# A rotation by 180 degrees on one core: a strip loaded first, and an early zero write to rows that the last store overwrites

## The chip, the cores and the metric

One core of a Trainium2 chip. The metric is the device time of one execution in microseconds. The kernel before takes 123.19 us (median of 3 runs, 123.14 to 123.35).

## The reference

```python
def setup_inputs():
    return {"x": np.random.randn(32, 3, 256, 256).astype(np.float32)}

def reference(x):
    return np.rot90(x, k=2, axes=(-2, -1)).astype(np.float32)
```

96 planes of 65,536 floats, each reversed end to end: 25.17 MB in, 25.17 MB out, no arithmetic.

## The kernel before

The 96 planes are three groups of 32. A group is 128 rows of 16,384 floats (64 KB): four rows to a plane, one row to a partition. A group is loaded whole, every row is reversed by DVE, and the store puts the four rows of each plane down in reversed order.

```python
    x4 = x.rearrange("b c h w -> (b c) (h w)").rearrange(
        "(g n) (s e) -> g (n s) e", n=G, s=4)
    o4 = out.rearrange("b c h w -> (b c) (h w)").rearrange(
        "(g n) (s e) -> g n s e", n=G, s=4)
    # ... buffers A, Bt, Ct of 64 KB a partition, T of 8 KB; cut
    def load(t, g, lo=0, hi=E):
        nc.sync.dma_start(out=t[:, lo:hi], in_=x4[g][:, lo:hi])

    def store(t, g):
        nc.sync.dma_start(out=o4[g][:, ::-1, :], in_=t[:, :])
    # across(dst, src): four DVE copies, reversed, from one buffer to another; cut
    # inside(t): twelve DVE copies that reverse a buffer in place through T; cut

    load(A, 0)
    load(Bt, 1)
    across(Ct, A)
    store(Ct, 0)
    load(A, 2)
    inside(Bt)
    store(Bt, 1)
    across(Ct, A)
    store(Ct, 2)
```

Of the kernel before, what the change touches and what calls it, by code (L numbers as in the profile page):

```python
# [2 lines left out]

os.environ.setdefault("NEURON_RT_ULTRASERVER_MODE", "4")

# [4 lines left out]


@with_exitstack
def kernel(
    ctx: ExitStack,
    tc: tile.TileContext,
    x: bass.AP,
    out: bass.AP,
):








    nc = tc.nc
    P = 128

    B, C, H, W = x.shape
    L = H * W
    G = 32
    E = L // 4
    K = E // 4
    J = E // 8

    x4 = x.rearrange("b c h w -> (b c) (h w)").rearrange(
        "(g n) (s e) -> g (n s) e", n=G, s=4)
    o4 = out.rearrange("b c h w -> (b c) (h w)").rearrange(  # L40
        "(g n) (s e) -> g n s e", n=G, s=4)

    pool = ctx.enter_context(tc.tile_pool(name="slots", bufs=1))
    A = pool.tile([P, E], x.dtype, tag="A")
    Bt = pool.tile([P, E], x.dtype, tag="B")
    Ct = pool.tile([P, E], x.dtype, tag="C")
    T = pool.tile([P, J], x.dtype, tag="T")

    def back(t, lo, hi):
        return t[:, hi - 1:(lo - 1 if lo else None):-1]  # L50

    def copy(dst, src):
        tc.keep_in_program_order(nc.vector.tensor_copy(out=dst, in_=src))  # L53
# [7 lines that stand above are left out]
    def across(dst, src):  # L61
        for c in range(0, E, K):
            copy(dst[:, c:c + K], back(src, E - c - K, E - c))

    def inside(t):
        for lo in range(0, E // 2, J):
            hi = E - lo - J
            copy(T[:, :], back(t, hi, hi + J))
            copy(t[:, hi:hi + J], back(t, lo, lo + J))
            copy(t[:, lo:lo + J], T[:, :])  # L70

    load(A, 0)
    load(Bt, 1)
    across(Ct, A)
    store(Ct, 0)
# [7 lines that stand above are left out]
# [1 line left out]
_INS = ['x']  # L84
_OUTS = [((32, 3, 256, 256), 'float32')]


# [23 lines left out]
```

## Time and profile before

| | before |
|---|---|
| time, span in the profile | 123.19 us, 121.26 us |
| one DMA queue's share of 16 engines' span | 97.3% |
| DVE busy | 27% |
| a normal packet (65,536 B) on one DMA engine | 2.418 us |

Each of the 16 DMA engines carries six transfers of eight packets, back to back. A *round* is one packet on each of the 16 engines, a *turn* is the place where the queue changes from loads to stores or back, and a *ring* is the queue of one issuing engine, q1 of SyncE and q10 of ACT on the pages below. Where a packet takes longer than 2.42 us, I call the difference its *excess*; averaged over the 16 engines, it is 0.67 us in the first packets of the first load and 1.12 us in the last packets of the second load, just ahead of the first store. I call the latter "the slow round". The lines of the page and of the stretches stand in the prediction. They are cut so that each stretch holds one packet of every engine; a packet's bytes and its time count where it starts. The same holds for the DMA row of the page: a low digit says that few packets start in that slice, not that the engines stand still.

### The profile page before, as it was taken

How to read it: one execution, taken by the hardware profiler on the slowest of the kernel's cores; microseconds unless marked ns; L12 is line 12 of the kernel's file. 1: busy time of each engine (PE TensorE's matmuls, PEld its weight loads, DVE VectorE, ACT ScalarE, POOL GpSimd, SP SyncE). 2: the span in 40 equal slices, each digit the busy share in tenths (PEclk: the TensorE clock that was granted, in tenths of full speed). 3: DMA queues.
4: the chain of work that ended last, by engine and by line, in shares of the span. 5: the costliest groups of instructions: out<-in, count | busy, mean ns of one | idle time of the engine just before them, and what ended most of it. 6: DMA issues, size and time to landing. Idle time of an engine off the chain costs nothing.

```text
span 121.3 us, 72 instructions
## 1 busy us (share of the span) xinstructions
DVE 32.5 (27%) x20; POOL 0.2 (0%) x4
## 2 busy tenths in 40 slices
DVE  0000000599300079999100000009990000000000
POOL 0000000000000000000000000000000000000000
DMA  9777977997899497799789977997798779877980
GB/s 346 346 346 346 692 346 346 389 649 346 346 432 605 195 497 346 346 605 432 346 346 605 432 346 346 627 411 346 346 649 389 346 346 649 389 346 346 670 368 0
DMA packets 864, 50.33 MB, mean 415 GB/s; under 512 B 96, under 2 KB 96, under 8 KB 96
## 3 DMA queue, kind: packets, MB, share of 16 engines
q1 hardware_dynamic: 864, 50.33, 97.3%
HBM read 25.17 MB, written 25.17 MB: 415 GB/s over the span
## 4 chain that ended last, share of the span: by engine, by line
DMA 59%; DVE 13%; DVEq 2%; SPq 1%; issue 0%
DMA A<-in_x_dram 59%; DVE Ct L53 13%; DVEq L106 2%; SPq L59 1%; DVEq L53 0%
## 5 line engine op out<-in xcount | busy, mean ns | idle before, releaser
L53 DVE COPY Ct<-A 128x4096 f32<-128x4096 f32 x8 | 17.8, 2288 | 46.3 <-DMA A<-in_x_dram 46.3
L53 DVE COPY T<-Bt 128x2048 f32<-128x2048 f32 x4 | 4.9, 1228 | 11.7 <-DMA Bt<-in_x_dram 11.6
L53 DVE COPY Bt<-Bt 128x2048 f32<-128x2048 f32 x4 | 4.9, 1227 | 0.1
L53 DVE COPY Bt<-T 128x2048 f32<-128x2048 f32 x4 | 4.9, 1226 | 0.1
L95 POOL MEMSET const-bfloat16-1.0<- 128x1 bf16 x1 | 0.1, 102 | 0.0
L95 POOL MEMSET const-uint8-127<- 128x1 uint8 x1 | 0.1, 101 | 0.0
L95 POOL MEMSET const-float32-0.0<- 128x1 f32 x1 | 0.1, 99 | 0.2 <-issue 0.2
L95 POOL MEMSET const-float32-1.0<- 128x1 f32 x1 | 0.1, 98 | 0.0
## 6 DMA issues: line engine op xcount, KB each, us to landing
A<-in_x_dram SPq DMA_DIRECT2D x2, 35.7
out_dram<-Ct SPq DMA_DIRECT2D x2, 30.3
Bt<-in_x_dram SPq DMA_DIRECT2D x1, 41.9
out_dram<-Bt SPq DMA_DIRECT2D x1, 42.9
```

What stands on the lines that cost most here:

```text
L53: tc.keep_in_program_order(nc.vector.tensor_copy(out=dst, in_=src))
L59: nc.sync.dma_start(out=o4[g][:, ::-1, :], in_=t[:, :])
L95: nc = _bacc.Bacc("TRN2", target_bir_lowering=False, num_devices=1)
L106: with _tile.TileContext(nc) as tc:
```

## The change

Its intent, as far as the text shows it: a strip of 2 KB of every row goes first, so that the engines start on short packets; and 512 B of every output row of the last group are written with zeros at once, on ACT's ring, so that the output has been written to early. The last store overwrites the zeros.

```diff
+    Z = 128
+    N = E // 32
+    z4 = out.rearrange("b c h w -> (b c) (h w)").rearrange(
+        "(g n) (s e) -> g (n s) e", n=G, s=4)
 ...
-    load(A, 0)
+    zeros = T[:, 0:Z]
+    nc.vector.memset(zeros, 0.0)
+    load(A, 0, 0, N)
+    load(A, 0, N, E)
+    nc.scalar.dma_start(out=z4[2][:, 0:Z], in_=zeros)
     load(Bt, 1)
```

## The prediction

> **What bounds the kernel now.** I read the page first: engines, then the queue, then the slices. DVE is busy 27% of the span and no other engine computes, while the one DMA queue is busy for nearly all of it:
>
> ```profile
> span 121.3 us, 72 instructions
> DVE 32.5 (27%) x20; POOL 0.2 (0%) x4
> DMA  9777977997899497799789977997798779877980
> ...
> q1 hardware_dynamic: 864, 50.33, 97.3%
> ```
>
> Columns of the last line: packets, MB, share of 16 engines' span. 50.33 MB is the whole input read once and the whole output written once, so no byte can be saved. The lone "4" in the DMA row (slice 14, about 39.4 to 42.5 us) is the only weak slice between the first and the last. Next, does the queue ever wait for DVE? The SyncE waits and the timeline answer it:
>
> ```profile
> SPq L106 <- DMA out_dram<-Ct: 19.3, 1, 19.3
> ...
> 31.50 0.63 SPq L59 DMA_DIRECT2D out_dram<-Ct  x1
> ...
> 58.22 0.55 SPq L59 DMA_DIRECT2D out_dram<-Bt  x1
> ...
> 90.86 0.54 SPq L59 DMA_DIRECT2D out_dram<-Ct  x1
> ```
>
> The timeline's columns are start and length of the issue in us. In the trace's packet records the three stores' first packets start near 42.4, 81.1 and 100.4 us, so each store was issued about 10 to 23 us before its turn. DVE is off the path, and the chain of waits on the page (which goes through DVE copies) is not what sets the end. What sets it is the slowest of the 16 DMA engines, each of which carries 6 transfers x 8 packets of 65,536 B without a gap.
>
> So I cut the span at packet boundaries (columns: stretch, length, DVE, POOL, clock, DMA share, GB/s):
>
> ```profile
> 0.00:1.70 1.70, 0.00 (x0) 0.20 (x4) 1.00 0.00 0
> 1.70:4.70 3.00, 0.00 (x0) 0.00 (x0) 1.00 1.03 350
> 4.70:7.10 2.40, 0.00 (x0) 0.00 (x0) 1.00 1.01 437
> 36.20:38.60 2.40, 0.00 (x0) 0.00 (x0) 1.00 1.01 437
> 38.60:42.10 3.50, 0.00 (x0) 0.00 (x0) 1.00 1.01 300
> 42.10:44.50 2.40, 1.38 (x2) 0.00 (x0) 1.00 1.01 437
> ```
>
> Each stretch from the second on holds one packet per engine (16 x 65,536 B). The normal round takes 2.4 us at 437 GB/s. Two rounds don't: the first load's first packet (3.0 us) and the last packet of the second load, just ahead of the first store (3.5 us). The packet records say it per engine: a normal packet is 2.418 us and the pace is 19.319 us for eight, 2.415 each. The first packets start between 1.74 and 2.70 us and take 2.60 to 3.31 us. The last packets of the second load take 3.30 to 3.97 us, a mean of about 1.13 us too much, on all 16 engines together. No later turn between load and store, in either direction, has such a packet (largest 2.494 us). The engine that ends the kernel (its last landing record at 120.12 us) is the one with the largest stall, 3.969 - 2.419 = 1.55 us. From there to the end of the span is 1.14 us, and from the span to the measured time 123.19 - 121.26 = 1.93 us.
>
> Budget: start to first packet 1.94, first packet 3.02, 46 normal ones 46 x 2.415 = 111.09, the stalled one 3.97, tail 1.14: 121.16 of 121.26; the rest is semaphore packets and a 0.08 us slow packet at 79 us.
>
> **What the Trainium skill says.** "DMA: Bandwidth & Descriptors", section "Where 436 GB/s comes from", gives 16 ports x 32 B x 850 MHz = 435 GB/s as the ceiling; the full rounds above, at about 435, agree. So the normal packets can't get faster, and only the two slow rounds and the start are to be had. The same page, "Issuing engines are not separate DMA queues": what ACT issues runs on the same 16 engines and interleaves with SyncE's. This trace has no ACT transfer, so it can't say. Its section "Queues, rings and completion order" says that an engine takes turns between rings at packet boundaries, and that a DMA's semaphore is the ordering one has; so the 512 B zero packets will be mixed into the first load, and the overwriting store must wait for the zeros' semaphore, which will be some 95 us old by then. "HBM Reference", section "Latency", has 0.2 us on average and 2 us at high load; the two engines that started last show a first packet of 2.604, 0.19 us over normal, which fits the 0.2. No page that I found speaks of a stall at the first write to a tensor; that reading of the 3.5 us round is my own inference.
>
> **The change, part by part.** The intent must be the two slow rounds. The engines that began at 1.74 us waited longest and those that began at 2.5 to 2.7 us hardly at all, as if one thing, ready at about 2.6 us, let all reads go. The 3.5 us round looks like the same for the output's first write. The zero write makes that first write at 2 to 3 us, where engines stand still anyhow.
>
> - *Removed: the stall at 38.6 to 42.1.* Taking each engine's excess off its own end, the last engine is then the one that started at 2.70 us: its last packet ends near 119.72, with 0.89 us of stall, so 118.83. Against 120.12 this is a gain of 1.29 us, not 1.55, because another engine becomes the last.
> - *Added: the strip.* The same bytes in 16 packets per engine rather than 8 for the first load. A packet's fixed share is 2.415 - 65,536 B / 27.2 B per ns (the skill's 435 by 16, an estimate) = 6 ns, up to 10. Eight more packets and a 9 ns semaphore packet: 0.06 to 0.1 us. It also adds a SyncE issue of about 0.4 us (the first two took 0.38 and 0.42) but eight strip packets (8 x 2,048 B / 27.2 = 0.6 us) cover that. The first packet's latency is paid as before; I see no direct gain from the strip, other than that zeros need not wait behind a 2.4 us packet.
> - *Added: the zeros.* 8 packets per engine of 512 B: 19 ns of bytes plus 10 ns, 0.24 us at least; I take 0.3 as an estimate, since short writes may cost more. The memset of 128 elements on DVE, by the copies' 1.23 us for 2,048, is under 0.1 us, beside other work. ACT's issue then comes at about 1 us; SyncE's first took 1.0 us from issue to first packet, so zeros move from about 2.1 us on.
> - *Moved: the first write's stall.* If it is still about 1.1 us from about 2.1 us on, it ends at 3.2 to 3.4, where reads flow from 2.6 to 2.9. If it blocks the engine, as it blocked a load's packet in the kernel before, some 0.5 us stays exposed; if it blocks only its own ring, none. I take 0.3.
> - *Unmoved:* DVE's copies, whose slack is 10 us; T is needed again only at 43 us.
>
> Sum: -1.29 + 0.1 + 0.3 + 0.3 = -0.6, so 122.6. I say **122.5**, leaning a little to a fuller hiding.
>
> **Rivals.** (a) *The stall is hidden fully*, with zero packets running inside the wait for the first read: -1.29 + 0.1 = 122.0, and 121.7 if the strip also lets the late engines start sooner (their 0.3 us). For it: the read stall is there anyway. Against: engines that start late have no idle time to give. (b) *The stall is not about the first write* but about the first load-to-store turn on SyncE's ring, or hits each region of the output when it is first touched, and the zeros touch the wrong one. Then it stays at about 39 us and the added packets cost 0.2 to 0.6: 123.4 to 123.8. Against: stores to the second and third part show no stall in the kernel before, so one first touch serves the whole output. (c) *It is given back in full*: the stall comes at the start and blocks all engines one after the other with the read stall: -1.29 + 1.13 + 0.4 = 123.4. For it: it was a load's packet that was lengthened, so such a stall can hold up other work on the engine. (d) *Zeros are far dearer than their bytes*, say 0.2 us each: 8 x 0.2 = 1.6 less the 0.3 assumed puts it at 123.8.
>
> **Range and chances.** (a) gives the low end, (b) and (c) the high: 121.7 to 123.5. A gain over 2% needs 120.73, a cut of 2.46 us; taking out both slow rounds whole (1.3 and at most 0.9) doesn't reach it. A loss of 2% needs 125.65, which only (d) several times over could bring. Hence 0.02, 0.96, 0.02.
>
> **What would show it.** Right: no round over 2.5 us near 39 us, all later rounds near 2.4 us at 435 GB/s, a first load that lands later than 22.55 us by 0.3 to 0.8 us, and the second load's landing at 43.07 coming forward by over 0.5 us. Wrong: a 3.5 us round that is still just ahead of the first store (b); the first load landing later by over 1.2 us (c, d); or a first load that lands no later than before (a). DVE on the path at any store would refute the whole frame.

## The result, and the profile after

123.1 us (median of 4 runs, 123.05 to 123.2) against 123.16 (4 runs, 123.02 to 123.35); the ratio is 0.9995, interval 0.9977 to 1.0012. The time is the same. It lies inside the stated range of 121.7 to 123.5, but 122.5 was forecast, a gain of about 0.7 us, and there is none. The page of the changed kernel (slices of 3.03 us, the two queues and their issues):

```profile
span 121.3 us, 79 instructions
...
DMA  4977997998889297799789977997798779877980
...
q1 hardware_dynamic: 1008, 50.33, 97.2%
q10 hardware_dynamic: 144, 0.07, 0.2%
...
out_dram<-T ACTq DMA_DIRECT2D x1, 64.0 KB, 2.9
```

The zeros are queue q10, 144 packets: 128 of data and 16 of the semaphore, landed 2.9 us after their issue. The weak slice, "4" before, is now a "2", at the same place, slice 14: a few packets fewer happen to start in it, so this is no sign of a longer stall. The stretches of the changed kernel (stretch, length, DVE, POOL, clock, DMA share, GB/s) show the slow round itself:

```profile
36.20:38.60 2.40, 0.00 (x0) 0.00 (x0) 1.00 1.01 437
38.60:42.20 3.60, 0.00 (x0) 0.00 (x0) 1.00 0.97 291
42.20:44.60 2.40, 1.28 (x2) 0.00 (x0) 1.00 1.01 437
```

The slow round is untouched. Its packets take 3.26 to 3.90 us, mean excess 1.09 us against 1.12. And the zeros had met no stall of their own. From the packet records of the changed kernel (times in us from the start of the span; the records don't name their engine; a packet is taken to follow the one at whose end it starts):

```
strip packets (2,048 B):  first at 1.74; 95 of the 128 take 0.081 to 0.087, the others up to 0.87
zero packets (512 B):     128 of them, from 2.73 to 3.53, every one 0.027 long, 0.0234 from start to start
first long packets:       start at 2.92 to 3.53, mean excess 0.04
semaphores of the zeros:  landed 3.26 to 3.89
last of the first load:   landed 22.79 (22.55 before)
second load:              landed 43.16 (43.07 before)
last semaphore packet:    starts at 120.07 (120.12 before), landed 120.46 (120.46 before)
```

So the output was written, and the write confirmed, by 3.9 us, in 27 ns a packet, and the turn at 39 us cost what it had cost before.

### The profile page after: what moved, and what is told of

Its sections match the earlier page's. It is cut to its first block, busy times and chain, and to the rows that moved or that the text cites. A ratio compares the mean times of both kernels' runs of the same rounds, so it can differ in the third digit from the quotient of the medians.

```text
span 121.3 us, 79 instructions
## 1 busy us (share of the span) xinstructions
DVE 32.7 (27%) x21; POOL 0.2 (0%) x4
## 3 DMA queue, kind: packets, MB, share of 16 engines
q1 hardware_dynamic: 1008, 50.33, 97.2%
## 4 chain that ended last, share of the span: by engine, by line
DMA 58%; DVE 13%; DVEq 2%; SPq 1%; issue 0%
DMA A<-in_x_dram 58%; DVE Ct L62 13%; DVEq L119 2%; SPq L68 1%; SPq L65 0%; DVEq L62 0%
```

## The experiments

Eighteen kernels. Those executed once are judged by their records. "Before" in a comparison is the kernel before on the same chip.

**The first four: later, earlier, on the other ring, to other rows.**

```diff
 # e1_reload
     load(Bt, 1)
+    load(Bt, 1)
 # e2_store_first
-    load(Bt, 1)
     across(Ct, A)
     store(Ct, 0)
+    load(Bt, 1)
 # e3_zeros_sp (the change, without the strip)
-    load(A, 0, 0, N)
-    load(A, 0, N, E)
-    nc.scalar.dma_start(out=z4[2][:, 0:Z], in_=zeros)
+    load(A, 0)
+    nc.sync.dma_start(out=z4[2][:, 0:Z], in_=zeros)
 # e4_zeros_g0 (the change)
-    nc.scalar.dma_start(out=z4[2][:, 0:Z], in_=zeros)
+    nc.scalar.dma_start(out=z4[0][:, 0:Z], in_=zeros)
```

> The kernel before with the second load issued twice, so the first store comes one load later (about 63 to 64 us instead of 42.4; the second load waits for the first's semaphore, some 2 us of empty queue near 43 us). Theory TURN (the slow round belongs to the last load packet before the first store, whatever the time): no packet over 2.6 us near 39 us, and packets of 3.3 to 4.0 us near 60 to 63 us. Rival CLOCK (something at a fixed time, 39 to 42.8 us after the start): 3.3 to 4.0 us at 39 us as before, nothing near 61 us. Rival ADDRESS (the last rows of the second load's data are slow to read): 3.3 to 4.0 us in both places.

> The kernel before with the second load moved behind the first store, so that the queue is empty from 22 to about 33 us and the store is then followed by loads; about 10 us slower. TURN: no packet over 2.6 us at 39 to 43 us; the stall shows at the store's first packet (3 us or more) or not at all, as no load is ahead of it. CLOCK: the packet that covers 39 to 42.8 us takes 3.3 to 4.0 us though it is a store's or the load's first. ADDRESS: the last packet of the moved load, about 69 us, takes 3.3 to 4.0 us.

> The change without the strip, and the zeros issued by SyncE between the first and the second load, to the same rows of the last group. RING (a form of TURN: the first store on SyncE's own ring costs it, and ACT's ring did not count): the last packet of the first load, about 18 to 22 us, takes 3.3 to 4.0 us, and the one at 39 us 2.42. If it is not the ring (region or time or size): 39 us slow as before, 2.42 at 20 us.

> The change with the zeros written to the first group's rows, those that the first real store writes, instead of the last group's. REGION (each region of the output costs at its first touch and the change touched the wrong one): the round at 39 us falls from 3.5 to 2.42 us and the time to about 122.0 to 122.5. All other theories: the slow round stays, 123.1 us.

*e1* and *e2* were inconclusive: the framework's scheduler moved the instructions. In e1 SyncE issued the store ahead of the repeated load (142.67 us), in e2 its instruction order came out as that of the kernel before (123.07 us), so e2 is a repeat of it. The moral is to look at the order of the built program first; the later runs either pin it or, as their issues in the trace show, came out in the order written.

*e3*: 123.52 us, before 123.34. With the zeros between the first and second load on SyncE's own ring there is no packet over 2.6 us near 20 us, and the slow round at 39 us keeps a mean excess of 1.02 us. *e4*: 122.99 us, before 123.34, slow round 1.12 us. So it is neither the ring nor the rows: the theory that the first write pays, whichever form, had no support left at this size of write.

**What the slow round goes with: time, address or place.** The loads and stores are now pinned to program order (a wrapper round both `dma_start` calls, except in e6, whose issues came out in the order written).

```diff
 # e5_delay
+    nc.vector.memset(A[:, :], 0.0)
     load(A, 0)
 # e6_groups_120: groups handled in the order 1, 2, 0
 # e7_store_in_order: e2's edit, pinned
 # e8_three_loads: e1's edit, pinned
```

> The kernel before with the loads kept in order behind a DVE memset of the whole buffer A, so that every transfer starts some 8 to 17 us later (call it D). CLOCK (a fixed time after the start): the slow round stays at about 38.7 to 42.7 us, now four to seven packets earlier in the second load, and the kernel takes 123.2 + D. PLACE (anything tied to what the queue does: packet count, turn, address): the slow round moves to 38.7 + D.

> The kernel before with the three groups handled in the order 1, 2, 0. ADDRESS OF THE INPUT (the last rows of group 1 are slow to read): the slow round moves to the last packets of the first load, about 18.6 to 22 us. Otherwise it stays at 38.7 to 42.7 us and the time at 123.2.

> What e2_store_first was meant to be (there the scheduler put the load ahead again): the second load is kept behind the first store, the queue is empty from 22 to about 33 us, time about 133. TURN: the first store's first packet, near 33 us, takes over 3 us, or nothing does, since no load packet is ahead of it; none near 39 us. CLOCK: the packets that cover 39 to 42.7 us, the first store's third and fourth, are slow by about 1 us. PACKET COUNT (after 16 data packets on an engine): the last packet of the store, about 50 us, is slow.

> What e1_reload was meant to be: two loads into the second buffer in order, then the first store, some 2 us empty near 43 us, time about 144.5. TURN: the slow round is just ahead of the first store, near 60 to 64 us, and none at 39. CLOCK, PACKET COUNT and ADDRESS: it stays at 38.7 to 42.7 us; ADDRESS has it again at 60 to 64 us, for the same rows are read again.

*e5* (140.26 us): everything begins 17.2 us later, and so does the slow round, at 55.8 to 60.0 us with 1.08 us. No fixed time. *e6* (123.0 us): the slow round stays at 38.7 us with 1.10 us although other rows are read there. No address of the input. *e8* (144.8 us), its stretches:

```profile
38.60:41.00 2.40, 0.00 (x0) 0.00 (x0) 1.00 1.01 437
57.90:60.30 2.40, 0.00 (x0) 0.00 (x0) 1.00 1.01 437
60.30:63.90 3.60, 0.00 (x0) 0.00 (x0) 1.00 0.99 291
63.90:66.30 2.40, 1.34 (x2) 0.00 (x0) 1.00 1.01 437
```

Nothing at 39 us now. The slow round (1.14 us) sits in the last packet of the third load, ahead of the first store, which has moved there. It belongs to the first turn from loads to stores. (The third load had to wait for the second to land. No packet runs for 1.28 us near 42 us, and the third load's first packets have 0.72 us of excess. Gaps like this are taken up below.)

*e7* (134.37 us) fitted no theory neatly. Its first store finds an empty queue and its first packets have 0.08 us of excess: a first big write on its own is not slow. But the turn from that store to the load behind it cost 0.75 us in the store's last packet (and 0.40 us in the next packet on eight engines), and the next turn, load to store near 92 us, 0.55. In the kernel before the same kind of turn, store to load at 62 us, costs nothing.

**Pattern, size, number of turns, two rings.**

```diff
 # e9_plain_store (wrong result on purpose: rows not exchanged)
-        nc.sync.dma_start(out=o4[g][:, ::-1, :], in_=t[:, :])
+        nc.sync.dma_start(out=z4[g], in_=t[:, :])
 # e10_big_zeros (the change, without the strip)
-    Z = 128
+    Z = E // 8
 # e11_more_turns: load(Bt,1), load(A,2) and all stores in column halves, pinned, in the order
 #   load A | load Bt lo | store | load Bt hi | store | load A lo | store | load A hi | store store store
 # e12_store_act
-        nc.sync.dma_start(out=o4[g][:, ::-1, :], in_=t[:, :])
+        nc.scalar.dma_start(out=o4[g][:, ::-1, :], in_=t[:, :])
```

> The kernel before with stores that write the rows in the order of the buffer's partitions (a wrong result on purpose), so that store and load split over the engines alike. PATTERN (the slow round is the price of the store's reversed three-level pattern, or of its other split over the engines): no packet over 2.6 us at 38.7 to 42.8 us, time about 122. TURN of any kind: slow round unchanged, mean excess 1.0 to 1.1 us, time 123.1 to 123.3.

> The change without the strip and with zeros of 8 KB a row instead of 512 B (1 MB, through ACT's ring, beside the first load). FIRST WRITE, ONLY TOO SMALL BEFORE: the 39 us round falls to 2.42 us and packets of the first load show the 1 us instead; about 125.5 (2.4 us of bytes more, less 0, as the cost moves). TURN: the 39 us round keeps its 1.0 to 1.1 us; about 125.6 to 126.

> The kernel before with the second and third load and all stores in column halves, so that SyncE's ring turns from load to store three times and back twice or more. EVERY TURN COSTS: 0.5 to 1.1 us of excess at each of the turns to a store (about 32, 52 and 71 us), time 125 or more. FIRST TURN ONLY: about 1.1 us at the first turn, near 29 to 32 us, under 0.2 us at the others, time 123.2 to 123.5.

> The kernel before with the stores issued on ACT's ring, so that no ring turns and loads and stores alternate packet by packet from about 32.5 us on. TURN WITHIN A RING: no slow round at all, about 122.0. FIRST LARGE STORE, whatever ring: packets with about 1 us of excess near 32 to 36 us, time 123.0 to 123.3. MIXING costs more than the turn: many packets over their pace, over 123.5.

*e9* (123.16 us, before 123.08; its result is wrong): slow round 1.22 us; the store's pattern doesn't matter. *e11* (123.26 us), stretches at the first, second and third turn to a store:

```profile
29.00:30.30 1.30, 1.30 (x2) 0.00 (x0) 1.00 0.98 378
30.30:32.20 1.90, 1.23 (x1) 0.00 (x0) 1.00 1.08 276
32.20:33.50 1.30, 0.00 (x0) 0.00 (x0) 1.00 1.00 429
50.60:51.80 1.20, 0.00 (x0) 0.00 (x0) 1.00 1.02 437
69.90:71.10 1.20, 0.00 (x0) 0.00 (x0) 1.00 1.01 437
```

Packets are 32 KB here and a normal one takes 1.213 us; the first stretch misses one of the 16 packets of its round. The first turn costs 0.13 and 0.84 us in two rounds, 0.97 together; the second 0.01 us near 50.8 us, the third nothing near 70 us, the fourth 0.07 us near 90 us. The price is paid once, not per turn.

*e12* (123.16 us median of 4 runs, 123.02 to 124.3; ratio 1.0036, interval 0.9983 to 1.0089): with the stores on ACT's ring the slow round comes as soon as the first store joins, in the load packets that start at 33.8 to 34.4 us, 1.24 us, and never again, though from there loads and stores alternate packet by packet. Not a matter of one ring.

*e10* (125.4 us): here an early write did change something. With 8 KB a row, mixed into the first load, the turn costs 0.44 us instead of 1.1, but the load's packets that start near 21.5 us, behind which two zero packets follow each other, have 0.31 us of new excess, and the zeros' own 8 x 0.309 = 2.47 us come on top. So size counts: 512 B pieces leave the turn as it is, 8 KB pieces lower it. But most of that is moved, not saved: over all rounds from the second to the turn the excess is 0.88 us, against 1.15 in the kernel before.

**Paid once per kernel, or once per stretch of work in the queue?** This decides what the price is. For the gap, the third load waits until the first store has landed.

```diff
 # e13_idle_between (pinned): the third load goes to C, behind a memset of C
-    load(A, 2)
     inside(Bt)
+    nc.vector.memset(Ct[:, :], 0.0)
+    load(Ct, 2)
     store(Bt, 1)
-    across(Ct, A)
-    store(Ct, 2)
+    across(A, Ct)
+    store(A, 2)
 # e17_short_gap: e13 without the memset
 # e18_gap_same_buffers (pinned): the kernel before, and
-    load(A, 2)
     inside(Bt)
+    nc.vector.memset(Ct[:, 0:8], 0.0)
+    nc.vector.memset(A[:, 0:8], 0.0)
+    load(A, 2)
```

> The kernel before with the third load put into buffer C behind a memset of C, so that the queue stands empty from about 62 to 77 us; then a load of 19.3 us turns to the second store near 97 us. STREAM STATE (an empty queue undoes what the first turn paid): 0.7 to 1.2 us of mean excess in the load's last packet near 93 to 97 us, besides the 1.1 us near 39 us. ONCE PER KERNEL (something that is touched once): under 0.2 us near 97 us. Total about 138 to 140 us either way.

> e13_idle_between without the memset of C: the third load into C still waits for the first store to land, so the queue is empty for 1.5 to 2.5 us near 62 us, and the turn to the second store comes near 83 us. If any empty moment resets the stream: 0.5 us or more of mean excess in the load's first packets near 64 us and 0.7 to 1.4 us in its last near 81 to 84 us, total about 126 to 127 us. If only a long rest does: under 0.2 us near 83 us, total about 125 us.

> The kernel before with its own buffers; two memsets of 8 elements make the third load (into A) wait until the first store has landed, so the queue is empty for 1 to 2 us near 62 us. If the gap is what brings the price back: 0.5 to 0.7 us of mean excess in the third load's first packets and 1.0 to 1.4 us in its last, near 81 to 85 us, total about 127. If the buffer did it in e17_short_gap: under 0.2 us at the turn, total about 125.2.

In the kernel before, the second load-to-store turn, at 81 us, costs nothing (one packet of 2.494 us). The stretch with the eight rounds of the third load, from just behind the first store to that turn:

```profile
61.40:80.70 19.30, 0.00 (x0) 0.00 (x0) 1.00 1.00 435
```

*e13* (143.96 us): the queue is empty from 62 to 80 us. Then the load's first packets have a mean excess of 0.56 us, as at the start of the kernel, and its last packets, at the turn to the second store, 1.40 us. *e17* (126.93 us, before 123.17): a gap of 1.30 us between the last packet of the store and the first of the load is enough, 0.53 and 1.24 us. *e18* (127.83 us, before 123.31) has the buffers of the kernel before and the gap alone; its stretches:

```profile
62.40:63.90 1.50, 0.08 (x2) 0.00 (x0) 1.00 0.00 0
63.90:66.80 2.90, 0.00 (x0) 0.00 (x0) 1.00 1.06 362
66.80:69.20 2.40, 0.00 (x0) 0.00 (x0) 1.00 1.01 437
78.90:81.30 2.40, 0.00 (x0) 0.00 (x0) 1.00 1.01 437
81.30:85.00 3.70, 0.00 (x0) 0.00 (x0) 1.00 1.01 283
85.00:87.40 2.40, 0.68 (x1) 0.00 (x0) 1.00 1.01 437
```

An empty stretch, a slow first round (0.66 us), normal ones, and a slow round at the next turn (1.33 us). So nothing is "touched once". An empty queue of 1.3 to 1.5 us brings both prices back, long after the first third of the output had been written. The time adds up: in e18 an engine stands idle for 2.64 us on average and then loses 0.66 and 1.33 us, 4.63 together, and the kernel is 4.52 us slower.

Three checks from the records. The pinning isn't the cause: e5 is pinned and has no gap at this place, and its second load-to-store turn has 0.01 us of excess. The length of the load ahead of the turn isn't either: in e1 two loads, 16 packets on each engine, run without a gap between the first and the second store, and that turn has 0.03 us. And the price of the restart is that of a load: in e7 the first packets behind a gap of 10.6 us are a store's, with 0.08 us.

**Where the cost of the added packets went.**

```diff
 # e14_strip_only: the change without the memset and the ACT store
 # e15_zeros_only: the change with load(A, 0) whole
 # e16_early_piece: no zeros; the last 8 KB of each row of group 0 loaded first,
 #   reversed, and stored through ACT's ring during the rest of the load
```

> The change without zeros. If the strip has no use of its own: eight packets of 84 ns and one semaphore packet in place of 8 x 76 ns cut from the long ones, 0.07 us later on every engine and 123.1 to 123.3. If it draws the engines' starts together (the change's spread of 0.52 us after the slow round against 0.62 before): 0.1 to 0.2 us faster, 122.9 to 123.0.

> The change without the strip. The zeros' packets are 8 x 27 ns and 9 ns on each engine, 0.23 us, and nothing hides them: 0.2 us slower, 123.3. If the zeros wait in the shadow of the first read: no change.

> No zeros; the last 8 KB of every row of the first group are loaded first, reversed and stored through ACT's ring while the rest of the load runs; no added bytes. If early mixing pays part of the first turn, as e10_big_zeros hints (excess at the turn 0.44 instead of 1.1, and 0.31 elsewhere): 122.7 to 123.0. If not: 123.2 to 123.4, for the added packets.

Against the kernel before (median of 11 runs 123.09 us): *e14* 123.01 us (6 runs), ratio 0.9999 (0.997 to 1.0028); *e15* 123.28 us (6), 1.001 (0.9987 to 1.0032); *e16* 122.93 us (6), 0.9985 (0.9958 to 1.0013). None is told from the kernel before by its time. The packet records tell a little more. Means over the 16 engines of one profile each, us from the start of the span; the first three rows do the same work up to this point, so they show the scatter:

| kernel | packet ahead of the turn starts | its excess | ends | latest engine's end |
|---|---|---|---|---|
| before | 38.87 | 1.12 | 42.41 | 42.77 |
| e2 (= before), e6, e9, e13 | 38.93, 38.90, 38.81, 38.87 | 1.01, 1.10, 1.22, 1.15 | 42.35, 42.42, 42.46, 42.43 | 42.67, 42.79, 42.82, 42.72 |
| e1, e17, e18 (= before up to the turn) | 38.95, 38.90, 38.82 | 1.04, 1.24, 1.39 | 42.41, 42.57, 42.63 | 42.93, 42.99, 43.60 |
| e14, strip alone | 38.77 | 1.30 | 42.49 | 42.74 |
| e15, zeros alone | 39.04 | 1.07 | 42.53 | 42.78 |
| after, e4 (both) | 39.02, 39.01 | 1.09, 1.12 | 42.52, 42.55 | 42.80, 42.73 |

With the zeros, alone or with the strip, the packet ahead of the turn starts at 39.01 to 39.04 us, later than in any of the first eight (38.81 to 38.95, mean 38.88): the added packets do cost the average engine about 0.14 us. With the strip alone it starts at 38.77, a little ahead of all eight. But at the end of the slow round nothing can be told apart any more: every excess and every mean end lies in the range of the eight (1.01 to 1.39, 42.35 to 42.63). That the strip's saving was paid back at the turn, with 1.30 us, is therefore not shown. At the end of the kernel the latest engine, which sets the time, is not later: its last packet ends at 120.08 us (after) and 120.03 (e4), against 120.07 to 120.24 in before, e2, e6 and e9, and the ends of the 16 engines lie within 0.52 and 0.53 us instead of 0.70 to 0.78. *e16* has the shape of e10: 0.72 us at the turn, 0.31 us new in the first load's last packets, and 1.24 us over all rounds up to the turn, no less than the kernel before's 1.15. The price was spread, not lowered.

No version beat the kernel before clear of noise.

## Why the prediction was wrong, point by point

- **What bounds the kernel**: right. DMA packets back to back, DVE aside; the changed kernel's queue has 97.2% of the span. Two readings were off without weight in the sum: 120.12 us is the last packet, the last landing was at 120.46; and the 0.19 us of the two engines that started last, set beside a latency of 0.2 us, is no constant, for in e1, e5, e8 and e12 the engine that started last has no excess (2.415 us).
- **"Removed: the stall at 38.6 to 42.1", -1.29 us**: this step failed. It rested on "the 3.5 us round looks like the same for the output's first write", marked as an inference. The zeros wrote to the output at 2.7 to 3.5 us at 27 ns a packet, and the slow round stayed, with 1.09 us instead of 1.12: the term measured -0.03 us, within the scatter. In its place the runs show a price of 1.0 to 1.4 us for the first large turn between loads and stores after the queue was empty (e5, e8, e11, e18); in e7, where the queue restarts with a store, it is split over two turns. The argument that misled me was sound as far as it went, "no later turn has such a packet", but once per kernel and once per unbroken run of the queue look alike in a kernel whose queue never runs dry. Only a gap could tell them apart.
- **"Moved: the first write's stall", +0.3 us**: there was nothing to move. The zeros ran from 2.73 us, not 2.1, at 27 ns each, and the first long packets behind them have 0.04 us of excess: no stall is seen beyond that of the first reads.
- **"Added: the zeros", 0.3 us**: 8 x 27 ns and a 9 ns semaphore packet, 0.225 us by the lengths of the records, or about 0.19 by their starts, 23.4 ns apart; near the 0.24 worked out. The mean engine came to the turn about 0.14 us later, the latest engine ended the kernel no later. The memset took 0.17 us, not under 0.1, beside other work.
- **"Added: the strip", 0.06 to 0.1 us**: 8 packets of 84 ns and 9 ns more, less 8 x 76 ns cut from the long ones, 0.07 us by the lengths, or about 0.04 by the starts, 80 ns apart. No such cost can be seen: with the strip alone (e14) the engines came to the turn 0.1 us sooner. Its "no direct gain" is right in the time.
- **The sum**: -0.6 became -0.06 in the medians, which is noise. Rival (b), that the stall is the first turn and stays, named the right event, though it isn't bound to SyncE's ring (e12), but put the time at 123.4 to 123.8, since it added the packets' cost to the engine that ends last. The latest of the 16 engines, with which the kernel ends, was not delayed: their spread at the end was 0.52 us instead of 0.70. Why the spread shrank is open.
- **The chances and the signs**: 0.96 for within 2% came out, and the time lies in the range, but neither speaks for the mechanism: the range's high end was made of rivals (b) and (c), in which nothing is gained. The second load landed 0.09 us later instead of over 0.5 earlier, the first 0.24 later (0.3 to 0.8 forecast). The observable that I named as fatal to the step ("a 3.5 us round that is still just ahead of the first store") is what the profile showed.

What stays open: why the first turn costs 1.0 to 1.4 us and later ones do not, what holds that state, why pieces of 512 B leave it as it is while 8 KB pieces spread it over earlier rounds, and what sets the split in e7. The runs with a gap (e13, e17, e18) were executed once each. Whether start and turn share one fixed sum is not shown either.

## What to carry to other kernels

A cost that a kernel shows once may be paid once per kernel or once per unbroken run of the queue; before building a warm-up for it, put a gap in and see whether it comes back. In a kernel bound by the DMA engines, don't let the queue run empty in mid-kernel: here gaps of 1.3 and 1.5 us (e17, e18) cost 1.8 and 2.0 us more in the rounds behind them. And read the packets of all 16 engines: the end is set by the latest, so a small cost on the mean engine can be free, and a small gain too.

## What the Trainium skill lacked or had wrong

- "DMA: Bandwidth & Descriptors", section "Latency and other measured facts" (and no other page that I found): nothing on the first change between loads and stores after an empty queue. Here it took 1.0 to 1.4 us on the mean of 16 engines, in the packet ahead of the first store (e5, e8, e9, e13, e18) or, with two rings, where the first store joins (e12: 1.24 us), and 0.00 to 0.08 us at later turns to a store without a gap (e2, e9, e11; e7 is apart, with 0.75 and 0.55 us at its first two turns).
- Same page, same section: no word on restarting a queue. After an empty stretch of 1 to 18 us the first packets of a load took 0.53 to 0.72 us too long on average (e8, e13, e17, e18), as at the start of the kernel (0.67 us before); those of a store 0.08 (e7).
- Same page, section "Where 436 GB/s comes from": agrees. Rounds without excess move 16 x 65,536 B in 2.415 us, 434 GB/s.
- Same page, section "Specifications" (512 B as the least for line rate): 512 B stores started every 23.4 ns where they ran in a row, 22 GB/s on an engine, against 27 GB/s in long packets; at its bound the rate is about 80% of the line's. 2,048 B loads, every 80 ns, had 94%.
- Same page, section "Issuing engines are not separate DMA queues": agrees. Moving all stores to ACT's ring (e12) gave a ratio of 1.0036, interval 0.9983 to 1.0089.
